# One term of the edge keys on GpSimd, key sums in PSUM, the activation table ahead of the loads, and another cut of the index arrays

## The chip, the cores and the metric

The kernel runs on one core of a Trainium2 chip. The metric is device time in microseconds: the median of several executions, and beside it the time of one profiled execution. The engines are TensorE (PE in the profile, its weight loads PEld), VectorE (DVE), ScalarE (ACT), GpSimd (POOL) and SyncE (SP); each runs its own instructions in order and waits on semaphores for the others. SyncE, ScalarE and GpSimd issue DMAs.

## The reference

```python
def reference(nodes, edges_src, edges_dst, w_msg, w_self):
    # nodes [4096, 256] f32, edges [262144] i64, weights [256, 256] f32
    self_out = nodes @ w_self
    msg = nodes[edges_src] @ w_msg
    agg = np.zeros((N, D), dtype=np.float32)
    np.add.at(agg, edges_dst, msg)
    return (self_out + agg).astype(np.float32)
```

Each of 262144 edges adds one row of `nodes @ w_msg` to the row of its destination.

## The kernel before

Every edge becomes one number, a key made of its destination's segment, its source's block of 128 and remainders of both. The keys are laid out as 128 partitions by 2048 columns and sorted by VectorE (min and max of columns that stand apart by a given distance, line 974), with turns of the layout through TensorE (line 1100) and ScalarE's copies (line 1104) between rounds. When the keys are sorted, VectorE makes one-hot matrices from them (lines 564 and 601), TensorE counts edges per destination and source block into a ring in PSUM (line 628), ScalarE copies the counts out (line 655), and TensorE multiplies them with the projected nodes (line 718). Stores go out from GpSimd.

The change lies in the first 20 us. The order of instructions on each engine is that of the program text (a manual schedule).

- The index arrays come in five pieces of columns, `PIECES` (line 67). SyncE issues the load of each piece's destinations `d64` (line 222), ScalarE that of the first four pieces' sources `s64`, SyncE that of the fifth (line 224). All are 64-bit; the lower halves are read with a stride.
- For each piece (lines 239 to 261) ScalarE makes three conversions: `seg` (line 244, from `d`), `blk` (line 247, from `s`) and `dst_p` (line 250, from `d`). VectorE then runs four instructions: `seg * step + blk` (line 253), the minimum with a bound plus `dst_p` (line 254), `low = blk * c + s` (line 255), and the sum of both (line 259), which is the key. `seg` and `blk` lie in `XS[0]` and `XS[1]`, the sums in the sort's buffers `XA[0]` and `XA[1]`, all in SBUF. The first sort instruction of line 974 reads the keys of all pieces.
- ScalarE's activation table is loaded in front of its first activation, so behind the four loads that it issues.
- GpSimd fills constants (lines 229 to 291) and runs 111 small memsets for a table (line 298), which SyncE sends to memory and reads back (lines 300 and 301). Then GpSimd issues the loads of the weights and the nodes (lines 305 to 313); the first of them is made to wait for `loaded`, the last conversion of the last piece. A cast of the identity follows (line 314). TensorE turns the nodes with it (line 349).

Of the kernel before, what the change touches and what calls it, by code (L numbers as in the profile page):

```python
# [9 lines left out]
P = 128  # L10
FP32 = mybir.dt.float32
BF16 = mybir.dt.bfloat16
I32 = mybir.dt.int32
# [4 lines left out]
ALU = mybir.AluOpType  # L18
AX = mybir.AxisListType
ACTF = mybir.ActivationFunctionType  # L20

BW = 512
SEG = 384
SHORT = 256
# [11 lines left out]
PARTS = 2  # L36
# [9 lines left out]
FP = 96  # L46
# [17 lines left out]
FILL = {8: 10, 32: 3}  # L64
PSUM0 = 0x2000000
SENT = float(1 << 24)
PIECES = (512, 512, 480, 320, 224)
TOP = 32767
SORT_A = [
    ('b', 419, 0),  # L70
# [59 lines left out]
def kernel(  # L130
# [9 lines left out]
    nc = tc.nc  # L140

    N, D = nodes.shape
# [3 lines left out]
    NCOL = E // P  # L146
    assert NCOL == 2048
    T = N // P
    G16 = NCOL // P

    const = ctx.enter_context(tc.tile_pool(name="const", bufs=1))
# [18 lines left out]
    ident = const.tile([P, P], FP32, name="ident")  # L170
    make_identity(nc, ident[:])

    wcat = feat.tile([P, 4, D], BF16, name="wcat")
# [5 lines left out]
    stt = nc.vector.scalar_tensor_tensor  # L179
# [7 lines left out]
    XA = [sortp.tile([P, FP + NCOL + BP], FP32, name=f"XA{i}") for i in range(2)]  # L187
    XS = [sortp.tile([P, TOT], FP32, name=f"XS{i}") for i in range(2)]
    id2 = sortp.tile([P, 2 * P], FP32, name="id2")
    id_bf = sortp.tile([P, P], BF16, name="id_bf")  # L190
# [5 lines left out]
    def muladd(out, in_, m, a):  # L196
        return nc.vector.tensor_scalar(
            out=out, in0=in_, scalar1=float(m), scalar2=float(a), op0=ALU.mult, op1=ALU.add
        )

    tab = const.tile([P, G16], I32, name="tab")
    per, per_short = SEG * NCOL // N // NB, SHORT * NCOL // N // NB
    ahead = FULL * (per - per_short)
# [12 lines left out]
    ld = []  # L216
    j = 0
    for h, m in enumerate(PIECES):
        d64 = ldp.tile([P, m], I64, name=f"d64_{h}")
        s64 = ldp.tile([P, m], I64, name=f"s64_{h}")  # L220
        c = slice(j, j + m)
        nc.sync.dma_start(d64[:], edges_dst.rearrange("(p j) -> p j", p=P)[:, c])
        q = nc.scalar if h < 4 else nc.sync
        q.dma_start(s64[:], edges_src.rearrange("(p j) -> p j", p=P)[:, c])
        ld.append((d64, s64, c))
        j += m
# [3 lines left out]
        nc.gpsimd.memset(x[:, FP + NCOL:], SENT)  # L230
    for h in range(2):
        nc.gpsimd.tensor_copy(out=id2[:, h * P:(h + 1) * P], in_=ident[:])
    seg = XS[0][:, 0:NCOL].bitcast(I32)
    blk = XS[1][:, 0:NCOL].bitcast(I32)
    dst_p = XR[0][:, 0:NCOL]
    step = SEG * (NB - 1) // (SEG - SHORT)
    top_b = (NSEG - 1 - 6) * step
    assert step * (SEG - SHORT) == SEG * (NB - 1) and TOT >= NCOL
    for d64, s64, c in ld:
        dlo = d64[:].bitcast(I32)[:, 0::2]  # L240
        slo = s64[:].bitcast(I32)[:, 0::2]
        key = XA[0][:, FP + c.start:FP + c.stop]
        low = XA[1][:, FP + c.start:FP + c.stop]
        nc.scalar.activation(
            out=seg[:, c], in_=dlo, func=ACTF.Copy, scale=1.0 / SEG, bias=0.5 / SEG - 6.5
        )
        nc.scalar.activation(
            out=blk[:, c], in_=slo, func=ACTF.Copy, scale=1.0 / P, bias=0.5 / P - 0.5
        )
        loaded = nc.scalar.activation(  # L250
            out=dst_p[:, c], in_=dlo, func=ACTF.Copy, scale=1.0 / (SEG - SHORT), bias=0.0
        )
        stt(out=key, in0=seg[:, c], scalar=float(step), in1=blk[:, c], op0=ALU.mult, op1=ALU.add)
        stt(out=key, in0=key, scalar=float(top_b), in1=dst_p[:, c], op0=ALU.min, op1=ALU.add)
        stt(
            out=low, in0=blk[:, c], scalar=float((SHORT - 1) * P), in1=slo, op0=ALU.mult,
            op1=ALU.add,
        )
        stt(
            out=key, in0=key, scalar=float((SEG - SHORT) * P), in1=low, op0=ALU.mult, op1=ALU.add  # L260
        )

    zer = const.tile([P, 3, P], BF16, name="zer")
    NAT = 20
    atr = const.tile([P, NAT, BW], BF16, name="atr")
# [10 lines left out]
    stgn = tc.alloc_tile_pool(name="stage_n", bufs=1)  # L276
# [13 lines left out]
    nc.gpsimd.tensor_copy(out=rows[:, 0:2 * NW], in_=jrow[:, ON_ACT:].rearrange("p k i -> p (k i)"))  # L290
    nc.gpsimd.tensor_copy(out=rows[:, 2 * NW:], in_=drow[:, 0:NW].rearrange("p k i -> p (k i)"))
    nc.sync.dma_start(kd[0:1, NCOL:NCOL + 1], ones_sent[:])
    c = 0
    for n, wid, gap in GROUPS:
        z = slice(c // GP, (c + n) // GP)
# [5 lines left out]
    nc.sync.dma_start(  # L301
        by_q[:], tab_d.rearrange("o (t h q) -> q (o t) h", t=3, h=PARTS)
    )
    DEP = mybir.DependencyInfo(mybir.DependencyClass.Sync, mybir.DependencyReason.DATA)
    first = nc.gpsimd.dma_start(wcat[:, 0:2, :], w_self.rearrange("(k p) f -> p k f", p=P))
    tc.add_manual_dep(first.ins, loaded.ins.name, DEP, reason="edges first")
    nc.gpsimd.dma_start(wcat[:, 2:4, :], w_msg.rearrange("(k p) f -> p k f", p=P))
    nodes_bf = stgn.tile([P, T, D], BF16, name="nodes_bf")
    for t in range(0, T, T // PARTS):
        nc.gpsimd.dma_start(  # L310
            nodes_bf[:, t:t + T // PARTS, :],
            nodes[t * P:(t + T // PARTS) * P, :].rearrange("(b p) f -> p b f", p=P),
        )
    nc.gpsimd.tensor_copy(out=id_bf[:], in_=ident[:])

    psum_y = tc.alloc_tile_pool(name="psum_y", bufs=1, space=bass.MemoryType.PSUM)

# [131 lines left out]
    for t in range(GP // 4):  # L449
        tp = psum_sort.tile([P, 512], FP32, name="tp_sw", tag="tp", bufs=4)  # L450
        for k in range(4):
            c = (4 * t + k) * P
            nc.tensor.matmul(
                out=tp[:, k * P:(k + 1) * P], lhsT=own[:, c:c + P], rhs=ident[:],
# [5 lines left out]
    for t, tp in enumerate(tps):  # L460
        for k in range(4):
            nc.tensor.matmul(
                out=tp[:, k * P:(k + 1) * P],
# [4 lines left out]
            out=vals[:].rearrange("p (q k) -> p q k", k=GP)[:, :, 4 * t:4 * t + 4],  # L468
            in_=tp[:].rearrange("p (k q) -> p q k", k=4),
            func=ACTF.Relu, scale=-1.0, bias=top[:],  # L470
        )

    def load(c):
        regs = [nc.tensor.alloc_register(f"po{c}_{i}") for i in range(NREG)]
        h, q = divmod(c // NREG, P)
        nc.tensor.load(regs, poff[q:q + 1, h * GP:h * GP + NREG])
        return regs
# [3 lines left out]
    first = load(0)  # L481
# [145 lines left out]
    def count_mm(ap, lhsT, rhs, start, after=()):  # L627
# [6 lines left out]
        for i in after:  # L634
            tc.add_manual_dep(mm, i.name, DEP, reason="bank free")
        tc.add_to_no_dep_group("count", mm)
# [14 lines left out]
    def evac(r):  # L651
# [6 lines left out]
        )  # L658
        tc.add_manual_dep(ins, last_mm[0].name, DEP, reason="run complete")
        tc.add_to_no_dep_group("evac", ins)  # L660
# [133 lines left out]
    if True:  # L794
# [5 lines left out]
        c = 0  # L800
# [5 lines left out]
        for c in range(NCOL):  # L806
# [44 lines left out]
            for _ in range(FILL.get(c + 1, 0)):  # L851
                nc.tensor.matmul(
                    out=out_ps[:, 2:4, :], lhsT=zw[:, 0:P], rhs=zw[:], start=True, stop=True,
                    skip_group_check=True,
                )
            while nev < NRUN and (evac_at(nev) <= c or c == NCOL - 1):
# [6 lines left out]
                if stores and nev % 4 == 0:  # L863
                    dst, src = stores.pop(0)
                    tc.add_manual_dep(
                        nc.gpsimd.dma_start(out=dst, in_=src, accum_op=ALU.add).ins,  # L866
                        evac_of[nev].name, DEP, reason="pace",
                    )
# [350 lines left out]
```

## Time and profile before

| | |
|---|---|
| median of 3 runs | 418.43 us (417.76 to 420.45) |
| the profiled execution, its own time | 418.17 us |
| span of that execution, first to last instruction | 416.4 us |
| mean granted clock of TensorE | 0.978 of full speed |
| first VectorE key instruction | 7.56 us from the span's start |
| first sort instruction | 19.18 us |

Times in the views are microseconds from the start of the span unless they are marked ns. "Idle before" is the time for which an engine stood idle ahead of an instruction, and behind the arrow is what released it.

### The profile page before, as it was taken

How to read it: one execution, taken by the hardware profiler on the slowest of the kernel's cores; microseconds unless marked ns; L12 is line 12 of the kernel's file. 1: busy time of each engine (PE TensorE's matmuls, PEld its weight loads, DVE VectorE, ACT ScalarE, POOL GpSimd, SP SyncE). 2: the span in 40 equal slices, each digit the busy share in tenths (PEclk: the TensorE clock that was granted, in tenths of full speed). 3: DMA queues.
4: the chain of work that ended last, by engine and by line, in shares of the span. 5: the costliest groups of instructions: out<-in, count | busy, mean ns of one | idle time of the engine just before them, and what ended most of it. 6: DMA issues, size and time to landing. Idle time of an engine off the chain costs nothing.

```text
span 416.4 us, 10756 instructions
## 1 busy us (share of the span) xinstructions
PE 335.5 (81%) x4128; PEld 287.9 (69%) x4137; DVE 374.9 (90%) x916; ACT 270.0 (65%) x559; POOL 43.0 (10%) x172
## 2 busy tenths in 40 slices
PE   0038477876967198999999998898988999999995
PEld 0025255564845056999999998797878988898895
DVE  6999999999799989999999999989997999998851
ACT  4328154553538015889888888996876877777782
POOL 8400000000000000002011020100102030202010
PEclk9999699999999689999999999999999999999999
DMA  8690000101023200003012020230203020211212
GB/s 305 138 185 4 2 1 2 50 0 52 1 101 116 87 0 2 2 2 39 2 16 28 2 32 10 53 41 8 33 3 39 2 32 12 28 14 15 29 16 53
DMA packets 18074, 16.20 MB, mean 39 GB/s; under 512 B 3684, under 2 KB 16997, under 8 KB 18022
## 3 DMA queue, kind: packets, MB, share of 16 engines
q0 software_dynamic: 8992, 6.29, 12.7%
q1 hardware_dynamic: 8310, 7.20, 5.3%
q10 hardware_dynamic: 720, 2.00, 1.2%
q8 instruction: 34, 0.56, 0.6%
q14 instruction: 18, 0.15, 0.1%
HBM read 8.93 MB, written 8.66 MB: 42 GB/s over the span
## 4 chain that ended last, share of the span: by engine, by line
DVE 47%; PE 45%; issue 3%; ACT 3%; DMA 1%; DVEq 0%; ACTq 0%
DVE XA L974 18%; PE out_ps L718 18%; PE ring L628 17%; DVE e_oh L601 7%; PE tp_sw L1100 5%; DVE d_oh L601 5%; DVE XS L974 4%; DVE XR L974 3%; DVE off L564 3%; PE warm L994 2%; PE out_ps L725 1%; DMA d<-in_edges_dst_dram 1%; ACT XA L1104 1%; DVE atr L688 1%; ACT atr L655 1%
## 5 line engine op out<-in xcount | busy, mean ns | idle before, releaser
L655 ACT CAST atr<-ring 128x472 bf16<-128x472 f32 (+11 forms) x352 | 177.2, 553 | 45.7 <-PE ring L628 40.7
L718 PE MATMUL out_ps<-Y,atr 128*128 128x256 bf16 x1024 | 162.2, 272 | 2.9 <-DVE atr L688 2.0
L628 PE MATMUL ring<-d_oh,e_oh 128*128 128x88 bf16 (+9 forms) x2048 | 149.7, 203 | 9.9 <-issue 4.5
L628 PEld LDWEIGHTS <-e_oh 128*128 128x128 bf16 x2048 | 129.2, 97 | 16.4 <-issue 9.7
L718 PEld LDWEIGHTS <-atr 128*128 128x128 bf16 x1024 | 90.7, 97 | 10.8 <-DVE atr L688 2.3
L974 DVE TENSOR_TENSOR XA<-XA 128x510 f32<-128x510 f32 (+30 forms) x154 | 89.3, 630 | 6.9 <-ACT XA L1104 5.3
L601 DVE TENSOR_SCALAR e_oh<-off 128x1024 bf16<-128x1024 int16 (+5 forms) x254 | 87.0, 402 | 7.9 <-PE ring L628 5.2
L628 PE MATMUL ring<-zer 128*128 128x158 bf16 (+12 forms) x352 | 81.4, 231 | 0.1
L866 POOL DMA_DIRECT2D out_dram<-o_sb x30 | 28.9, 963 | 357.8 <-ACT atr L655 357.8
L601 DVE TENSOR_SCALAR d_oh<-off 128x1024 bf16<-128x1024 int16 (+5 forms) x204 | 63.9, 373 | 0.0
L1104 ACT COPY XA<-tp_sw 128x512 f32<-128x512 f32 x32 | 20.9, 654 | 41.5 <-PE tp_sw L1100 41.2
L1100 PE MATMUL tp_sw<-XA,id 128*128 128x128 f32 x256 | 36.7, 298 | 7.9 <-DVE XA L974 7.8
L1100 PEld LDWEIGHTS tp_sw<-XA,id 128*128 128x128 f32 x256 | 33.1, 194 | 13.7 <-DVE XA L974 8.7
L564 DVE TENSOR_TENSOR off<-pair,rows 128x2048 int16<-128x2048 int16 (+5 forms) x34 | 38.6, 1134 | 0.3
L628 PEld LDWEIGHTS <-zer 128*128 128x128 bf16 x352 | 34.1, 97 | 5.0 <-ACT atr L655 1.9
L994 PE MATMUL warm<-zw 128*128 128x512 bf16 x61 | 20.8, 440 | 17.5 <-DVE XS L974 9.3
L349 PE MATMUL x_ps<-id_bf,nodes_bf 128*128 128x128 bf16 x64 | 8.5, 304 | 29.3 <-DMA nodes_bf<-in_nodes_dram 28.0
L725 PE MATMUL out_ps<-Y,atr 128*88 128x256 bf16 (+7 forms) x115 | 31.2, 272 | 0.0
L688 DVE TENSOR_TENSOR atr<-atr 128x178 bf16<-128x178 bf16 (+24 forms) x100 | 23.7, 260 | 6.4 <-ACT atr L655 6.0
L349 PEld LDWEIGHTS <-nodes_bf 128*128 128x128 bf16 x64 | 6.6, 139 | 30.9 <-DMA nodes_bf<-in_nodes_dram 28.3
L321 PE MATMUL y_ps<-wcat,XT 128*128 128x256 bf16 x128 | 21.7, 278 | 6.9 <-ACT Y L325 2.8
L592 ACT ACTIVATE e_oh<-off,onesc 128x512 bf16<-128x512 uint16 (+5 forms) x36 | 24.6, 686 | 2.7 <-DVE off L564 2.7
(114 smaller groups left out, 223.3 us busy)
## 6 DMA issues: line engine op xcount, KB each, us to landing
out_dram<-o_sb POOLq DMA_DIRECT2D x30, 128.0 KB, 3.2
nodes_bf<-in_nodes_dram POOLq DMA_DIRECT2D x2, 1024.0 KB, 12.6
out_dram<-nodes_bf SPq DMA_DIRECT2D x4, 512.0 KB, 2.9
out_dram<-XA SPq DMA_DIRECT2D x4, 512.0 KB, 3.0
d<-in_edges_dst_dram SPq DMA_DIRECT2D x2, 512.0 KB, 5.5
s<-in_edges_src_dram ACTq DMA_DIRECT2D x2, 512.0 KB, 5.7
d<-in_edges_dst_dram SPq DMA_DIRECT2D x1, 480.0 KB, 9.6
s<-in_edges_src_dram ACTq DMA_DIRECT2D x1, 480.0 KB
```

The costliest lines, as they stand in the source:

```text
L564: tt(out=v[:, 0:n // 2].rearrange("p g w (k i) -> p (g w) k i", i=2), in0=pair[:, g].rearrange("p g w i -> p (g w) i").unsqueeze(2).to_bro ...
L601: ins = tss(out=o[:, 0:n // 2, j:j + m].rearrange("p g k i -> p g (k i)"), in_=v[:, 0:n // 2, w, 0:2 * m], scalar=float((-j0 if w else ON_ ...
L628: mm = nc.tensor.matmul(out=ap, lhsT=lhsT, rhs=rhs, start=start, stop=True, skip_group_check=True,).ins
L655: ins = nc.scalar.copy(out=at[:, 0:n], in_=ring[:, b:b + n]).ins
L688: tt(out=atr[:, j:j + n, 0:m], in0=atr[:, j:j + n, 0:m], in1=atr[:, i:i + n, at:at + m], op=ALU.add,)
L718: nc.tensor.matmul(out=out_ps[:, i, :], lhsT=at[:, t * P:(t + 1) * P], rhs=Y[:, b, :], start=(b == 0 and not last and t % 2 == 0), stop=(b ...
L725: nc.tensor.matmul(out=out_ps[0:m, 0, :], lhsT=spill[:, c0:c0 + m], rhs=Y[:, b, :], start=False, stop=False, skip_group_check=True,)
L866: nc.gpsimd.dma_start(out=dst, in_=src, accum_op=ALU.add).ins,
L974: self.nc.vector.tensor_tensor(out=out, in0=in0, in1=in1, op=op),
L994: self.nc.tensor.matmul(out=w[:], lhsT=self.zw[:, 0:P], rhs=self.zw[:], start=True, stop=True).ins
L1100: self.nc.tensor.matmul(out=tp[:, g * P:(g + 1) * P], lhsT=self.turned(rots[8 * h + 4 * t + g]), rhs=sel(x)[:, 4 * t + g], start=True, sto ...
L1104: self.nc.scalar.copy(out=sel(y)[:, 4 * t:4 * t + 4], in_=tp[:].rearrange("p (g i b) -> p g i b", g=4, b=bb),)
```

## The change

One short activation (`early_c`), on a cell that VectorE's first instruction sets to zero, stands ahead of the loads, so the table is loaded first. The pieces have other sizes, and ScalarE issues the sources of all but the first piece. Conversions run `blk`, `seg`, `dst_p`. For pieces 1 and 2 (counted from 0) GpSimd makes `low` with two instructions, and there `seg` goes to PSUM and `blk` to SBUF; for the others `low` stays on VectorE, `blk` goes to PSUM and `seg` to SBUF. The running sum `run` is in PSUM for all. The last sum of a piece (`finish_keys`) stands where `KEY_ORDER` says: a number is a piece's first part, a number with `~` its last sum. The weights and nodes wait for the fourth piece's last conversion, and GpSimd's small memsets and the table's transfers come behind them.

```diff
-PIECES = (512, 512, 480, 320, 224)
+PIECES = (256, 512, 512, 480, 288)
+ON_POOL = (1, 2)
+KEY_ORDER = (0, ~0, 1, 2, ~1, 3, ~2, ~3, 4, ~4)
...
+    early_c = const.tile([P, 1], FP32, name="early_c")
+    nc.vector.memset(early_c[:], 0.0)
+    nc.scalar.activation(out=early_c[:], in_=early_c[:], func=ACTF.Copy, scale=1.0, bias=0.0)
...
-        q = nc.scalar if h < 4 else nc.sync
+        q = nc.scalar if h else nc.sync
...
-    for d64, s64, c in ld:
...
+    def parts(h):
...
+        run = psum_k.tile([P, BW], FP32, name="run", tag="run", bufs=3)[:, 0:m]
+        held = psum_k.tile([P, BW], I32, name="held", tag="held", bufs=2)[:, 0:m]
+        seg, blk = (held, part[:, c]) if h in ON_POOL else (part[:, c], held)
...
+        low = XA[1][:, FP + c.start:FP + c.stop].bitcast(I32)
+        if h in ON_POOL:
+            nc.gpsimd.tensor_single_scalar(
+                out=low, in_=blk, scalar=(SHORT - 1) * P, op=ALU.mult
+            )
+            nc.gpsimd.tensor_tensor(out=low, in0=low, in1=slo, op=ALU.add)
+        else:
+            stt(
+                out=low, in0=blk, scalar=float((SHORT - 1) * P), in1=slo, op0=ALU.mult,
+                op1=ALU.add,
+            )
+        stt(out=run, in0=seg, scalar=float(step), in1=blk, op0=ALU.mult, op1=ALU.add)
+        stt(out=run, in0=run, scalar=float(top_b), in1=dst_p[:, c], op0=ALU.min, op1=ALU.add)
+        runs[h], lows[h] = run, low
+        return last
+
+    def finish_keys(h):
+        c = ld[h][2]
+        stt(
+            out=XA[0][:, FP + c.start:FP + c.stop], in0=runs[h],
+            scalar=float((SEG - SHORT) * P), in1=lows[h], op0=ALU.mult, op1=ALU.add,
+        )
+
+    for what in KEY_ORDER:
+        if what >= 0:
+            loaded = parts(what)
+            if what == len(PIECES) - 2:
+                near_end = loaded
+        else:
+            finish_keys(~what)
...
+    tc.add_manual_dep(first.ins, near_end.ins.name, DEP, reason="edges first")
```

## Rows read from the trace of the kernel before

**Rows 1.** The page's busy time by engine, with shares and instruction counts.
```profile
PE 335.5 (81%) x4128; PEld 287.9 (69%) x4137; DVE 374.9 (90%) x916; ACT 270.0 (65%) x559; POOL 43.0 (10%) x172
```

**Rows 2.** The chain that ended last, 0 to 60 us: start, length, what.
```profile
0.77 5.53 DMA d<-in_edges_dst_dram
...
19.18 1.02 DVE XA L974
```

**Rows 3.** Timeline of ScalarE: start, length, instruction, count, idle before and releaser.
```profile
0.77 2.60 ACTq L224 DMA_DIRECT2D s<-in_edges_src_dram  x4
3.39 1.28 ACT L244 ACT_TABLE_LOAD   x1 [3.39 <-issue]
6.32 0.66 ACT L244 ACTIVATE XS<-d 128x512 int32<-128x512 int32 x1 [1.64 <-DMA d<-in_edges_dst_dram]
6.88 0.64 ACT L247 ACTIVATE XS<-s 128x512 int32<-128x512 int32 x1
...
8.88 0.67 ACT L244 ACTIVATE XS<-d 128x512 int32<-128x512 int32 x1 [0.80 <-DMA d<-in_edges_dst_dram]
...
11.31 0.64 ACT L244 ACTIVATE XS<-d 128x480 int32<-128x480 int32 x1 [0.64 <-DMA d<-in_edges_dst_dram]
...
14.19 0.38 ACT L244 ACTIVATE XS<-d 128x224 int32<-128x224 int32 x1
```

**Rows 4.** Timeline of VectorE, pieces of 512, 480 and 224 columns.
```profile
7.56 0.69 DVE L253 SCALAR_TENSOR_TENSOR XA<-XS,XS 128x512 f32<-128x512 int32 x1 [2.65 <-ACT XS L247]
8.36 0.69 DVE L254 SCALAR_TENSOR_TENSOR XA<-XA,XR 128x512 f32<-128x512 f32 x1
8.97 0.68 DVE L255 SCALAR_TENSOR_TENSOR XA<-XS,s 128x512 f32<-128x512 int32 x1
9.69 0.69 DVE L259 SCALAR_TENSOR_TENSOR XA<-XA,XA 128x512 f32<-128x512 f32 x1
10.30 0.68 DVE L253 SCALAR_TENSOR_TENSOR XA<-XS,XS 128x512 f32<-128x512 int32 x1
...
13.02 0.65 DVE L253 SCALAR_TENSOR_TENSOR XA<-XS,XS 128x480 f32<-128x480 int32 x1
13.78 0.66 DVE L254 SCALAR_TENSOR_TENSOR XA<-XA,XR 128x480 f32<-128x480 f32 x1
14.35 0.65 DVE L255 SCALAR_TENSOR_TENSOR XA<-XS,s 128x480 f32<-128x480 int32 x1
...
17.54 0.38 DVE L253 SCALAR_TENSOR_TENSOR XA<-XS,XS 128x224 f32<-128x224 int32 x1
18.03 0.39 DVE L254 SCALAR_TENSOR_TENSOR XA<-XA,XR 128x224 f32<-128x224 f32 x1
18.34 0.38 DVE L255 SCALAR_TENSOR_TENSOR XA<-XS,s 128x224 f32<-128x224 int32 x1
18.75 0.39 DVE L259 SCALAR_TENSOR_TENSOR XA<-XA,XA 128x224 f32<-128x224 f32 x1
```

**Rows 5.** The DMA view from 4 to 12 us: all packets.
```profile
DMA packets 1048, 3.27 MB, mean 409 GB/s; under 512 B 117, under 2 KB 163, under 8 KB 1047
```

**Rows 6.** Waits of SyncE's queue, 0 to 20 us: total, times, longest.
```profile
SPq L222 <- DMA s<-in_edges_src_dram: 3.5, 1, 3.5
```

**Rows 7.** Timeline of SyncE, the issue behind its loads.
```profile
9.26 0.30 SPq L292 DMA_DIRECT2D kd<-ones_sent  x1
```

**Rows 8.** VectorE's only read of PSUM, groups by shape: busy us, mean ns, idle before.
```profile
L742 DVE COPY XR<-out_ps 128x256 f32<-128x256 f32 x1 | 0.4, 424 | 4.3 <-PE out_ps L718 4.3
```

**Rows 9.** GpSimd's groups by shape that read 128 columns.
```profile
L314 POOL CAST id_bf<-ident 128x128 bf16<-128x128 f32 x1 | 0.9, 945 | 0.0
...
L232 POOL COPY id<-ident 128x128 f32<-128x128 f32 x2 | 0.5, 298 | 0.0
```

**Rows 10.** Timeline of GpSimd, the first load of weights.
```profile
15.48 0.89 POOL L305 DMA_DIRECT2D wcat<-in_w_self_dram  x1 [5.26 <-ACT XR L250]
```

**Rows 11.** Timeline of TensorE, the first work behind the projected nodes.
```profile
47.08 2.56 PE L994 MATMUL warm<-zw 128*128 128x512 bf16 x5 [5.32 <-DVE XA L974]
```

## What I expect of the change, blind

> **What bounds the kernel now.** I read the busy shares first, then the chain of waits, then the timelines of the first 20 us engine by engine, since every edit lies there. VectorE is the busiest engine, 90% of the span [rows 1]. The chain begins with the landing of the first destination indices (0.77 to 6.30) and from 19.18 it is VectorE's sort [rows 2]. Between the two stand ScalarE's conversions and VectorE's twenty key instructions. The reader should see two clocks there. Loads: ScalarE starts the first three pieces at 6.32, 8.88 and 11.31, each released by a landing [rows 3]. VectorE: it starts at 7.56 and issues four instructions for each piece without a gap to 19.18 [rows 4]. A piece of 512 columns takes it 2.74 us (7.56 to 10.30, the next piece's first start, which is one spacing of 0.61 behind 9.69), and the loads bring one in 2.56. So VectorE follows the loads closely, and what is taken from it can turn into waiting for data. That is what the sum has to decide. The sort behind it is one chain of VectorE work, so a shift of its start goes through to the end.
>
> **The table load and the smaller first piece.** ScalarE issues four loads from 0.77 to 3.37, then loads its table for 1.28 us, then is idle for 1.64 until the first destinations land [rows 3]: the table load costs nothing now. Moved ahead, it stands in front of the issues: 0.77 plus 1.28, plus one tiny activation (about 0.25, an estimate from the 0.38 of 224 columns, the smallest shape in [rows 3]), so the second piece's sources are issued at about 2.3. The tiny activation's memset goes ahead of VectorE's constants, about 0.1 us under the wait for data.
>
> When do pieces land? Destination landings at 6.32, 8.88 and 11.31 stand 512 and 480 columns apart: (11.31 - 6.32) / 992 = 5.0 ns for a column of both index arrays; all loads together ran at 409 GB/s [rows 5], so the pace is that of the transfers. The new pieces end at columns 256, 768, 1280, 1760 and 2048, on that line at 5.0, 7.6, 10.2, 12.6 and 14.05. Sources lag by a little: a SyncE issue was held until 9.26 by a source landing, when the destinations of the same piece had released ScalarE at 8.88 [rows 3, 7]. The third piece matters most. Its sources are the second load of ScalarE's queue. Before, the first 1024 columns of that queue landed by 9.24, 8.47 us behind the queue's first issue; the same columns behind an issue at 2.3 give 10.8, and the line plus 0.2 gives 10.4. I take 10.6, and keep both.
>
> [...]
>
> The tenth load now stands on ScalarE's own queue. The ninth load of the kernel before was held 3.5 us, until a load of the first piece had landed [rows 6], and I expect the same hold here, ahead of ScalarE's first conversion. It costs at most one issue, 2.60 / 4 = 0.65 us: the first conversion starts at 5.2 to 5.85. That is covered: VectorE's four instructions on 256 columns (some 0.42 us each, from 0.39 at 224) end by 8.1, and its next needs the second piece's two conversions, 7.8 + 0.57 + 0.65 = 9.0. If the cover were gone it would cost those 0.65.
>
> **What VectorE no longer does.** Two instructions of 512 columns go to GpSimd, at a spacing of 0.61 each: 1.2 us. The new order also parts some dependent pairs: starts are 0.80 and 0.72 apart where an instruction reads the one before it, 0.61 where not [rows 4]. Ten such pairs become seven, 3 x 0.15 = 0.4 us. With a start near 5.9 in place of 7.56, a count of VectorE's work alone would promise over 3 us.
>
> The data do not allow it. VectorE has two instructions for the second piece, from 9.05 to 10.5, and its next needs the third piece's two conversions: 10.6 + 0.57 + 0.65 = 11.8. It waits 0.9 us ahead of the second piece and 1.3 ahead of the third. From there twelve instructions remain, with the spacings of [rows 4] (512: 0.80 dependent, 0.61 free; 480: 0.76 and 0.57; 288, between the rows of 224 and 480: 0.56 and 0.48 dependent, 0.38 free, 0.45 to the sort): 0.80 + 0.61 + 0.61 + 0.57 + 0.76 + 0.57 + 0.61 + 0.57 + 0.38 + 0.56 + 0.48 + 0.45 = 6.97. The later pieces are in time: the fourth's first conversion is read at 13.8, and its data are due at 12.8; the fifth is read at 16.9 and is due at 14.3. Sort starts at 11.8 + 6.97 = 18.8, against 19.18: 0.4 us earlier (0.2 by the late landing, 0.6 by the early one).
>
> **Sums in PSUM.** All eighteen instructions now have one operand in PSUM. The trace has one VectorE read of PSUM: a copy of 256 columns took 424 ns [rows 8], while 224 columns from SBUF took 0.38 to 0.39 and 480 took 0.66 [rows 4], which is 0.42 for 256. So nothing is added, and I take nothing; a whole dependent spacing more (0.11 us) for each of the twelve would be 1.3 us, the upper bound. [...]
>
> **GpSimd's part.** Two instructions for each of two pieces. The nearest rows are copies of 128 columns at 298 ns, and a cast of as many at 945 ns that ran beside VectorE's sort [rows 9]. For 512 columns that is 1.2 to 3.8 us each. At 1.2 the first pair runs from 8.45 to 10.8 and the second from 11.2 to 13.6. VectorE wants them at 13.2 and 15.8, so it waits for neither. I take 1.2, since VectorE's key instructions now read one SBUF operand each, while the sort beside the slow cast reads two. [...]
>
> **What is moved.** The weights and nodes are released by the fourth piece's last conversion instead of the fifth's, about 0.7 us earlier than 15.48 [rows 10]. They feed TensorE's early work, which ended 5.32 us before its next job had to start [rows 11]: worth nothing, and covered if a late GpSimd delays it by as much. GpSimd's 111 small memsets now follow the nodes, and SyncE's two table transfers follow them; their reader comes only after the whole sort.
>
> **Rivals.** (A) VectorE is not starved, because its instructions or conversions are quicker than taken. The last data then bound it: 14.25 + 0.45 for the conversion + 0.38 + 0.56 + 0.48 + 0.45 = 16.6, so 2.6 us earlier and about 415.8. For it: 2.2 us of waits. Against it: those waits hang on transfers already at 409 GB/s. (B) ScalarE's queue starts late: issues held behind the table load for up to the 1.64 us that the trace shows idle there. At the full 1.64 the third piece lands at 12.2 and the sort starts at 20.4, 1.2 us later than now: about 419.6. It decides as soon as the issue is more than 0.4 us late. [...] (C) PSUM operands cost VectorE time: at half the upper bound, 0.65 us on twelve instructions, the start is 0.3 us later than now, about 418.7. (D) GpSimd is blocked beside VectorE as in the slow cast: four instructions at 3.8 us from 8.45 end at 23.6, and six VectorE spacings (3.0 us) follow, so the sort starts at 26.6: 7.4 us later, 425.8. It speaks from 1.8 us an instruction on, and passes 1% from about 3. Against it: one SBUF operand for VectorE.
>
> **Numbers.** The profiled execution took 418.17 around its span of 416.4, and the median of the runs is 418.43, so 0.26 more. 418.43 - 0.4 = 418.0. Chances: the forecast 0.58 (its own range 417.2 to 418.8), A 0.12, B 0.14, C 0.10, D 0.04, and 0.02 for a gain beyond A that I can't name. The range from 415.8 to 419.7 takes in A to C. About 1% (4.2 us) is what a measurement of this kernel can tell from no change: faster by more 0.02, within 0.94, slower by more 0.04 (D).
>
> **What would show it.** In the timeline of after: the first ScalarE load issue near 2.3 (B: up to 3.9); VectorE idle ahead of the first instructions of pieces two and three, released by ScalarE, about 1 us each (A: none); the last stretch of twelve without idle time, at today's durations (C: longer by 0.07 or more); GpSimd's four at about 1.2 us, done before the instructions that want them (D: VectorE waits on GpSimd); the first sort instruction near 18.8. The forecast is wrong if that start is off by more than 0.8, or if the rest of the kernel doesn't keep the shift.

## The result, and the profile after

The median is 421.42 us (420.73 to 422.23, six runs), against 419.01 for the kernel before in the same session: a ratio of 1.0066, 95% interval 1.0047 to 1.0085. The change makes the kernel 0.7% slower. That is within 1%, but above the predicted range (415.8 to 419.7) and 3.4 us from the forecast of 418.0. The profiled execution took 422.23 around a span of 420.4.

First the start. ScalarE's timeline of the kernel after: start, length, instruction, count, idle before and releaser.

```profile
0.74 1.28 ACT L205 ACT_TABLE_LOAD   x1 [0.74 <-PEq L1234]
0.92 1.34 ACTq L229 DMA_DIRECT2D s<-in_edges_src_dram  x3
2.04 0.20 ACT L205 ACTIVATE early_c<-early_c 128x1 f32<-128x1 f32 x1
6.93 0.33 ACTq L229 DMA_DIRECT2D s<-in_edges_src_dram  x1
7.31 0.40 ACT L284 ACTIVATE held<-s 128x256 int32<-128x256 int32 x1 [5.08 <-DMA s<-in_edges_src_dram]
...
9.65 0.62 ACT L287 ACTIVATE held<-d 128x512 int32<-128x512 int32 x1 [0.72 <-DMA d<-in_edges_dst_dram]
...
12.15 0.62 ACT L287 ACTIVATE held<-d 128x512 int32<-128x512 int32 x1 [0.74 <-DMA d<-in_edges_dst_dram]
...
15.44 0.45 ACT L287 ACTIVATE XS<-d 128x288 int32<-128x288 int32 x1
```

The issues of the second piece's sources did not wait for the table: three ran from 0.92, beside the load. But the small first piece, meant to come at 5.0, was taken at 7.31, and the destinations of the second and third at 9.65 and 12.15, where the line of 5.0 ns a column had 7.6 and 10.2. (The fourth issue, at 6.93, was held until the first piece had landed, its sources at 6.91, as foreseen; it stands between that landing and 7.31, and VectorE's work on the second piece did not wait for it.) VectorE's timeline of the same kernel:

```profile
7.75 0.42 DVE L300 SCALAR_TENSOR_TENSOR XA<-held,s 128x256 int32<-128x256 int32 x1 [2.93 <-ACT held L284]
...
10.31 0.70 DVE L304 SCALAR_TENSOR_TENSOR run<-held,XS 128x512 f32<-128x512 int32 x1 [0.79 <-ACT held L287]
11.12 0.70 DVE L305 SCALAR_TENSOR_TENSOR run<-run,XR 128x512 f32<-128x512 f32 x1
12.81 0.70 DVE L304 SCALAR_TENSOR_TENSOR run<-held,XS 128x512 f32<-128x512 int32 x1 [0.99 <-ACT held L287]
...
16.14 0.67 DVE L305 SCALAR_TENSOR_TENSOR run<-run,XR 128x480 f32<-128x480 f32 x1
...
18.80 0.47 DVE L305 SCALAR_TENSOR_TENSOR run<-run,XR 128x288 f32<-128x288 f32 x1
...
19.79 1.01 DVE L1005 TENSOR_TENSOR XA<-XA 128x815 f32<-128x815 f32 x1
```

Both waits of VectorE are there (0.79 and 0.99, predicted 0.9 and 1.3), released by ScalarE. From 12.81 nothing is idle: twelve spacings to 19.79 are 6.98 us, predicted 6.97. The sort starts 0.61 later than before [rows 2], not 0.4 earlier. (That start varies: over all profiles with the loads of before it is 18.79 to 19.18, with the loads of after 19.64 to 19.86. The 19.18 is the latest of its kind, so 0.6 to 0.9 is lost here.) GpSimd's timeline:

```profile
9.03 1.50 POOL L295 TENSOR_SCALAR XA<-XS 128x512 int32<-128x512 int32 x1 [2.61 <-ACT XS L284]
10.62 1.28 POOL L298 TENSOR_TENSOR XA<-XA,s 128x512 int32<-128x512 int32 x1
11.87 1.48 POOL L295 TENSOR_SCALAR XA<-XS 128x512 int32<-128x512 int32 x1
13.44 1.29 POOL L298 TENSOR_TENSOR XA<-XA,s 128x512 int32<-128x512 int32 x1
15.50 0.94 POOL L325 DMA_DIRECT2D wcat<-in_w_self_dram  x1 [0.78 <-ACT held L284]
```

Its last sum ends at 14.73, and VectorE reads it from 16.71 on, so VectorE never waited for GpSimd.

So 0.6 to 0.9 us of the loss is made before the sort. The spans differ by 4.0 in these two executions (420.4 and 416.4). About 1.1 us of that is the first turn through TensorE. The chains of waits, first of after, then of before:

```profile
50.25 3.39 PE tp_sw L1131 x16
```

```profile
49.63 2.29 PE tp_sw L1100 x16
```

The granted clock stood at 0.50 of full speed from 42.98 to 53.22 in after, and from 43.47 to 50.30 in before. The length of this stretch does not decide the time: among the experiments' profiles that record it, it ends at 51.03 in e2 (median 420.73) and at 52.27 in e16 (416.86), and of the six executions of after, the one with the highest mean granted clock (0.988) took 421.78 and one at 0.974 took 420.73. What remains arises late, in the counting stage. VectorE makes the one-hots' offsets there in 34 instructions (`off`, line 564 of before), which serve as marks: the delay of the same mark against before, in us, out of the timelines of some kernels, the experiments' among them (each is one execution):

| mark in before | 156.2 | 299.7 | 340.5 | 368.5 | 390.9 |
|---|---|---|---|---|---|
| after | +1.73 | +1.83 | +2.81 | +5.01 | +4.04 |
| e12, after once more | +1.53 | +1.68 | +1.14 | +3.51 | +3.29 |
| e10, after without one wait | +1.24 | +1.30 | +1.07 | +0.93 | +0.19 |
| e5, before with six warm-ups | -0.53 | -0.27 | -0.53 | -1.11 | -3.62 |
| e9, the same six later | +0.35 | +0.71 | -1.07 | -1.65 | -3.49 |
| e15, before with twelve | +0.34 | +0.63 | +0.25 | +0.74 | +0.61 |

For 144 us every row of the table is nearly flat: a shift is handed on there. (Three kernels outside the table, e4, e7 and e14, fall back by 1.6 us between 286.5 and 299.7; theirs are the only profiles with the granted clock at half there, for 3.4 us.) Between 300 and 391 us each row goes its own way, by up to 4 us, and what stood in a row at 299.7 does not tell where it ends. The windows view from 300 to 350 us (us, then busy time and instructions of PE, PEld, DVE, ACT, POOL, granted clock, DMA share, GB/s), before and after:

```profile
300.00:350.00 50.00, 45.87 (x684) 41.64 (x684) 44.84 (x133) 36.82 (x73) 5.89 (x6) 1.00 0.15 18
```

```profile
300.00:350.00 50.00, 44.36 (x656) 39.85 (x655) 44.02 (x133) 35.58 (x71) 6.19 (x6) 1.00 0.16 20
```

In these 50 us at full clock TensorE of after does 28 matmuls fewer (by the marks, its work lies 2 to 3 us further back). The waits in that window (total, times, longest) say at what. Before:

```profile
PE ring L628 <- issue: 2.0, 3, 1.2
PEld L628 <- issue: 2.6, 5, 1.4
PEld L718 <- issue: 1.2, 2, 0.7
```

After:

```profile
PE ring L659 <- issue: 3.5, 7, 1.3
PEld L659 <- issue: 5.0, 9, 1.4
PEld L749 <- issue: 0.3, 1, 0.3
```

"issue" is time in which TensorE waited for nothing that the profile shows. (PE and PEld rows lie over one another in time, so their totals are not added.) Neither the ring nor the one-hots were edited: the change put work only into the first 20 us.

### The profile page after: what moved, and what is told of

It reads as the page before. It is cut to its first block, busy times and chain, and to the rows that moved or that the text cites. A ratio compares the mean times of both kernels' runs of the same rounds, so it can differ in the third digit from the quotient of the medians.

```text
span 420.4 us, 10776 instructions
## 1 busy us (share of the span) xinstructions
PE 337.4 (80%) x4137; PEld 288.6 (69%) x4137; DVE 374.0 (89%) x915; ACT 270.1 (64%) x560; POOL 50.8 (12%) x176
## 4 chain that ended last, share of the span: by engine, by line
PE 47%; DVE 43%; issue 4%; ACT 2%; DMA 2%; SPq 0%; DVEq 0%; ACTq 0%
PE out_ps L749 19%; PE ring L659 19%; DVE XA L1005 18%; DVE e_oh L632 6%; DVE XS L1005 6%; PE tp_sw L1131 6%; DVE d_oh L632 4%; DVE off L595 3%; DMA d<-in_edges_dst_dram 2%; DVE XR L1005 2%; PE out_ps L756 2%; ACT XA L1135 1%; DVE atr L719 1%; PE warm L1025 1%; ACT atr L686 1%
## 5 line engine op out<-in xcount | busy, mean ns | idle before, releaser
L659 PEld LDWEIGHTS <-e_oh 128*128 128x128 bf16 x2048 | 129.2, 97 | 18.8 <-issue 12.1
L897 POOL DMA_DIRECT2D out_dram<-o_sb x30 | 31.8, 1060 | 355.7 <-ACT atr L686 355.7
L1131 PEld LDWEIGHTS tp_sw<-XA,id 128*128 128x128 f32 x256 | 34.2, 200 | 13.6 <-DVE XA L1005 8.6
```

What stands on the lines that cost most here:

```text
L659: mm = nc.tensor.matmul(out=ap, lhsT=lhsT, rhs=rhs, start=start, stop=True, skip_group_check=True,).ins
L1131: self.nc.tensor.matmul(out=tp[:, g * P:(g + 1) * P], lhsT=self.turned(rots[8 * h + 4 * t + g]), rhs=sel(x)[:, 4 * t + g], start=True, sto ...
```

## The experiments

Times are medians; each ratio is to the kernel before, run in the same session.

**Each part by itself.** The change with the nodes released by the last piece again (e1), with the old split of the sources over the queues (e2), without GpSimd (e3), and the kernel before with the early table alone (e8).

```diff
# e1, in after
-            if what == len(PIECES) - 2:
+            if what == len(PIECES) - 1:
# e2, in after
-        q = nc.scalar if h else nc.sync
+        q = nc.scalar if h < 4 else nc.sync
# e3, in after
-ON_POOL = (1, 2)
+ON_POOL = ()
# e8, in before
+    early_c = const.tile([P, 1], FP32, name="early_c")
+    nc.vector.memset(early_c[:], 0.0)
+    nc.scalar.activation(out=early_c[:], in_=early_c[:], func=ACTF.Copy, scale=1.0, bias=0.0)
```

> The changed kernel, but the weights and nodes wait for the last conversion of the fifth piece again. Theory nodes: TensorE's early work ends 0.7 us earlier than before (41.0 against 41.8), stands idle 6.26 us instead of 5.32 ahead of the warm-up matmuls, and so the first turn runs at half clock (3.39 us instead of 2.29). Then here the work ends some 1.2 us later than in the changed kernel, the first turn takes about 2.3, and the median falls by about 1.1, to 420.3. Rival, chance of phase: the time at which the clock rises does not hang on that gap; the first turn may fall either way and the median stays within 0.4 of 421.4.

> The changed kernel, but ScalarE issues the sources of the first four pieces and SyncE those of the fifth, as before; the table load stays ahead. Theory load order: SyncE's queue carries the destinations of pieces one and two behind both arrays of piece nought, beside ScalarE's queue that is already at piece one, so the third piece's destinations landed at 12.06 where I took 10.6. With the old split both arrays of piece nought land by about 5.2, the third piece's destinations by 10.4, VectorE's first instruction starts near 6.0 and the sort near 18.5 instead of 19.79: median about 1.2 lower, 420.2. Rival, GpSimd or PSUM: the start of the sort stays within 0.4 of 19.79.

> The changed kernel, but VectorE makes the term low of all pieces and GpSimd none; sums stay in PSUM, loads as in the changed kernel. Theory load order: VectorE waited 0.79 and 0.99 us for conversions ahead of pieces one and two. One of the two added instructions (piece one's) falls into the second wait, the other costs about 0.6: the sort starts at 20.2 to 20.5 and the median is 0.5 to 0.7 higher, about 422. Rival, GpSimd costs more than it saves: the sort starts no later than 19.8 and the median falls.

> The kernel before with one part of the change alone: the tiny activation, and so the table load, ahead of ScalarE's issues. The trace of the changed kernel shows the issues running beside the table load (from 0.92, the table from 0.74 to 2.02), so the loads and the sort's start stay within 0.1 of before and the median within 0.4 of 418.2. Rival, a cause behind the first 20 us: about 2 us of the changed kernel's loss are not in the start of the sort; if this part alone carries them, the median is 420 or more.

| run | time | ratio, 95% | sort starts |
|---|---|---|---|
| e1 | 420.44 | 1.0061 (1.0048 to 1.0074) | 19.83 |
| e2 | 420.73 | 1.0058 (1.0038 to 1.0079) | 19.40 |
| e3 | 421.75 | 1.0085 (1.0070 to 1.0099) | 19.77 |
| e8 | 418.23 | 1.0000 (0.9981 to 1.0019) | 18.78 |

None of the parts removes the loss. The early release of the nodes costs and brings nothing that the intervals show: e1's median is near the 420.3 expected, but the kernel before was faster in that session too, and the ratio is that of after. e2 took its first piece at 4.93, but its third only at 11.20, when the sources came, and its sort started at 19.40, not at the 18.5 expected. GpSimd's share saves nothing: e3 starts its sort at the same moment. Its VectorE timeline shows why:

```profile
9.44 0.68 DVE L300 SCALAR_TENSOR_TENSOR XA<-held,s 128x512 int32<-128x512 int32 x1
10.55 0.69 DVE L304 SCALAR_TENSOR_TENSOR run<-XS,held 128x512 f32<-128x512 int32 x1 [0.42 <-ACT XS L287]
...
11.96 0.68 DVE L300 SCALAR_TENSOR_TENSOR XA<-held,s 128x512 int32<-128x512 int32 x1
12.79 0.69 DVE L304 SCALAR_TENSOR_TENSOR run<-XS,held 128x512 f32<-128x512 int32 x1 [0.15 <-ACT XS L287]
```

The two instructions that came back to VectorE (9.44 and 11.96) fell into the waits, which shrank to 0.42 and 0.15. I had expected a start of 20.2 to 20.5 there; it was 19.77. The table alone (e8) brings nothing: its 18.78 is no more than the lower end of the starts that the loads of before give.

**The first turn.** If the half clock in the first turn were the cause, warm-ups that start earlier would mend it. Six more warm-up matmuls went ahead of the first turn (e4 in after, e5 in before, e7 in after with e2's split).

```diff
-WARM = [((2.7, 1.4), 3)] * 4 + [...]
+WARM = [((5.4, 4.0, 2.7, 1.4), 3)] + [((2.7, 1.4), 3)] * 3 + [...]
```

> The changed kernel, but the warm-up matmuls ahead of the first turn are four groups of three, begun some 2.7 us earlier (near 44.6 instead of 47.29). Theory clock: the first turn of the changed kernel ran at half clock until 53.22; with TensorE busy earlier the clock is full when the turn starts at 50.25, the turn takes about 2.1 instead of 3.39 and the median falls by 1.1 to 1.3, to about 420.2. Rival: the first turn is as long as before and the median stays within 0.4 of 421.4.

> The kernel before, with the same earlier warm-up groups ahead of the first turn as in the run e4_warm_early. That run was 3.1 us faster than the changed kernel, of which the late start of the sort is no part. Theory clock, same for both kernels: TensorE's granted clock rises at times that fall by chance against the warm-up, so the kernel before loses at its first turn as well in part of its executions, and this one gains 0.5 to 1.2: about 417.3. Theory clock, worse for the changed kernel: the first turn of the kernel before is at full clock nearly always, and this one stays within 0.4 of 418.2. If it gains as much as the changed kernel did (to about 415), the gain is not tied to the change at all.

> The changed kernel with the old split of the loads and the earlier warm-up together. Theory: the sort starts at 19.4, 0.2 later than before; the first turn is at full clock; the median lies 0.3 to 0.5 below the run e4_warm_early (sort at 19.64), near 417.9, so no faster than before by more than 0.5. Rival: the split costs elsewhere what it gains, and the median stays at 418.3 or above.

e4: 418.32 (1.0007, 0.9987 to 1.0027). e7: 418.74 (1.0000, 0.9974 to 1.0026). e5: 413.68 (0.9882, 0.9857 to 0.9907), the fastest kernel of this study and faster than both. e7 did not reach the 417.9 expected: the earlier start of its sort (19.50) brought nothing in the time. The gains (421.22 of e12 to 418.32 in after, 417.94 of its session to 413.68 in before) are too large for the first turn: e5 is 0.53 us earlier at the first mark and 3.62 at the last. So they too arise in the counting stage.

**The same six, ahead of the second turn** (e6 in after, e9 in before), where the clock of before is full anyway (from 50.30).

```diff
+WARM = [((2.7, 1.4), 3), ((5.4, 4.0, 2.7, 1.4), 3)] + [((2.7, 1.4), 3)] * 2 + [...]
```

> The changed kernel with the same six extra warm-up matmuls, but ahead of the second turn, where the granted clock is full anyway. Theory clock: no gain, median 421 to 421.8. Rival, TensorE's instruction supply: twelve more instructions ahead of the counting stage shift where its code arrives, and that, not the clock, gave the run e4_warm_early its gain; then this median falls to 419 or less.

> The kernel before with the six extra warm-up matmuls ahead of the second turn, where the granted clock is full. The run e5_before_warm gained 4.3 us with the same six ahead of the first turn, but its trace is only 0.53 us ahead where the counting stage begins, and the rest is gained behind 307 us. Theory code supply: what counts is where TensorE's instruction stream stands, twelve instructions further on, so this one gains most of it too: 415 or less, with the start of the counting stage within 0.5 of before. Theory clock: no gain, 417.5 to 418.5.

e6: 419.01 (1.0014, 0.9993 to 1.0036). e9: 415.20 (0.9922, 0.9897 to 0.9947). Most of the gain is there without any warmth to win. What the two places have in common is that all later instructions of TensorE stand twelve places further back in its program.

**One wait.** TensorE's program differs between before and after in one thing only: the sums in PSUM (`psum_k`) share banks with the later `psum_y`, so TensorE's first weight load waits on VectorE and ScalarE as well as on the nodes. That takes one instruction more at the head of its program; it is passed at 19.79 and TensorE's work begins at 26.92, so it delays nothing. (The pages' counts of all instructions show it: 10756 before and 10757 in e11, 10766 in e10 and 10767 in e12.) e10 gives `psum_y` banks of its own, in after; e11 adds such a wait to the kernel before; e12 is after with another comment.

```diff
# e10, in after: the pool's line moved up
+    psum_y = tc.alloc_tile_pool(name="psum_y", bufs=1, space=bass.MemoryType.PSUM)
     psum_k = tc.alloc_tile_pool(name="psum_k", bufs=1, space=bass.MemoryType.PSUM)
# e11, in before, at the first x_ps matmul
+                        for late_one in (loaded, keyed):
+                            tc.add_manual_dep(ins, late_one.ins.name, DEP, reason="one more wait")
```

> The changed kernel with the turns' PSUM pool laid out ahead of the key sums' pool, so the two don't share banks: TensorE's first weight load no longer waits for VectorE and ScalarE, and the one extra instruction that held these waits is gone from TensorE's stream. Theory code supply: that one instruction is the part of the loss behind the first 60 us, and the median falls by 1.5 to 2, to about 419.5. Rival: nothing changes, 421 to 421.8.

> The kernel before, with the same two waits (VectorE's last key, ScalarE's last conversion) on TensorE's first weight load: both have long passed when it runs, so no wait is longer, but TensorE's stream has one instruction more in front of everything. Theory code supply: 1.5 to 2 us slower, near 419.8. Rival: within 0.4 of 418.1.

> The changed kernel itself once more, beside the others on the same chip, to see how its first turn and its counting stage come out in another profiled execution. All theories: median 421 to 421.8. Theory clock chance: the first turn may be at full clock here (2.1 to 2.3 us) with the median no lower.

e10: 418.95 (1.0014, 0.9995 to 1.0033). e11: 419.57 (1.0038, 1.0023 to 1.0053). e12: 421.22 (1.0070, 1.0048 to 1.0091). Without the one instruction 2.3 us of the loss are gone, although the sort starts as late as in after (19.86); with it the kernel before loses 1.2 us. (e10 also changes the PSUM banks of some tiles, which no run tests apart; e11 changes none, so there the instruction stands alone.) The window from 300 to 350 us in e10:

```profile
300.00:350.00 50.00, 46.28 (x692) 41.90 (x690) 44.92 (x135) 37.15 (x73) 6.54 (x6) 1.00 0.16 18
```

This window is not the only place of the loss: e12 runs level with e10 at the mark 340.5 and loses behind it. Between the marks 354.5 and 368.5 the six kernels with the wait and without extra warm-ups all fall back against before, after by 1.8, e12 by 2.4, e1, e2, e3 and e11 by 0.8 to 2.0; the three others without it (e8, e10, e13) get ahead by 0.2 to 0.4. The late start of the sort does not divide them this way: e10 and e13 have it, e11 has not. The weight loads' waits there (total, times, longest) go the same way: before (352 to 370 us) and e10 (353 to 371), then after (355.5 to 373.5) and e12 (354 to 372):

```profile
PEld L628 <- issue: 1.3, 5, 0.4
```

```profile
PEld L658 <- issue: 1.6, 5, 0.6
```

```profile
PEld L659 <- issue: 2.5, 4, 1.2
```

```profile
PEld L659 <- issue: 3.1, 4, 1.4
```

**Warmth or place, and the landing.** Two and twelve more warm-ups in the kernel before (e14, e15), and all loads on one queue in e10, without (e13) and with the six (e16).

```diff
# e14: two more ahead of the second turn
+WARM = [((2.7, 1.4), 3), ((2.7, 1.4), 4)] + [((2.7, 1.4), 3)] * 2 + [...]
# e15: six more ahead of the second and of the third
+WARM = [((2.7, 1.4), 3)] + [((5.4, 4.0, 2.7, 1.4), 3)] * 2 + [((2.7, 1.4), 3)] + [...]
# e13, in e10; e16 is this with e6's edit
-        q = nc.scalar if h else nc.sync
+        q = nc.sync
```

> The kernel before with two more warm-up matmuls (four more TensorE instructions with their weight loads) ahead of the second turn; six there gave 3.2 us. If warmth is what gained: a third of that gain, 417.2 to 417.5, with the second turn shorter and the counting stage as before. If the place of the later instructions in TensorE's program is what counts: no third of anything; the waits put down to issue in the counting stage differ from before, their sum (before 10.5 and 4.5 us) moves with the time, and the time can be anywhere from 415 to 420.

> The kernel before with six more warm-up matmuls ahead of the second turn and six ahead of the third. If warmth is what gained: at least the 3.2 us of six, 413.5 to 415.2. If the place in TensorE's program counts: the gain is not kept by rule, 415 to 419, and its sum of issue waits in the counting stage lies between those of the kernel with six (time 415.2) and before by the same amount as the time.

> The changed kernel without the extra wait ahead of TensorE's first work (as in the run that takes it away), with all ten loads issued by SyncE, one behind the other, so that no second queue runs beside the first piece. If the late landing came from two queues that do not share the transfers equally: the third piece's destinations land at 10.2 to 10.8 instead of 12.1, the sort starts at 18.7 to 19.2 instead of 19.8, and the time is 418.0 to 418.4, 0.6 to 0.9 below the same kernel with two queues (418.95). If the transfers as a whole are simply slower with the smaller rows: the third piece lands near 12, the sort starts at 19.7 to 19.9 and the time stays at 418.9 to 419.1.

> The kernel with one load queue and without the extra wait, and six more warm-ups ahead of the second turn: TensorE's stream is the same as in the kernel before with those six (415.2). If place in TensorE's program counts, the gain of 3.2 carries over: 414.6 to 415.4, with the sort's start as in the run with one queue. If what the six gain depends on the data's timing instead, as the changed kernel with the six (419.0, a gain of 2.2 there) would have it: 415.8 to 416.4 or more.

| run | time | ratio, 95% | warm-ups more than before |
|---|---|---|---|
| e14 | 417.25 | 0.9962 (0.9935 to 0.9989) | 2 |
| e9 (above) | 415.20 | 0.9922 (0.9897 to 0.9947) | 6 |
| e15 | 420.44 | 1.0054 (1.0030 to 1.0078) | 12 |
| e13 | 419.66 | 1.0028 (1.0006 to 1.0050) | 0 |
| e16 | 416.86 | 0.9979 (0.9953 to 1.0006) | 6 |

Two fit warmth by the median (a third of six, 417.2 to 417.5), but not run by run: four of e14's twelve executions took 414.5 to 415.0 and the others 416.2 to 419.7, with one and the same program. Twelve refute it: 2.1 us slower than none, where warmth asked for 413.5 to 415.2. The windows view from 300 to 350 us, e9 and then e15:

```profile
300.00:350.00 50.00, 47.96 (x733) 44.31 (x731) 46.33 (x140) 38.91 (x78) 7.66 (x6) 1.00 0.16 18
```

```profile
300.00:350.00 50.00, 45.46 (x679) 41.43 (x680) 44.85 (x133) 36.11 (x72) 5.72 (x6) 1.00 0.15 18
```

Six put 49 matmuls more into these 50 us than the kernel before has, twelve 5 fewer. (The profiled execution of e15 took 418.41, near the 418.17 of before's, so it does not show the 2.1 us of the median.) That fits place. e16 was to reach 414.6 to 415.4 and came out at 416.86, outside it; but against its own base, e13 (419.66), six gained 2.8, nearly the whole 3.2. What was not kept is the base: e13, whose TensorE program is that of before, is 1.3 slower than before, of which its later sort (19.56) can be a part. So place alone doesn't set the time, and neither does it within one kernel, as e14 shows; what the other engines do at that moment may count too, which no run shows by itself.

e13 speaks on the landings. With one queue ScalarE's timeline has the pieces in order:

```profile
4.46 0.40 ACT L285 ACTIVATE held<-s 128x256 int32<-128x256 int32 x1 [2.22 <-DMA s<-in_edges_src_dram]
...
8.77 0.66 ACT L285 ACTIVATE XS<-s 128x512 int32<-128x512 int32 x1 [3.23 <-DMA s<-in_edges_src_dram]
...
11.36 0.67 ACT L285 ACTIVATE XS<-s 128x512 int32<-128x512 int32 x1 [0.84 <-DMA s<-in_edges_src_dram]
11.94 0.60 ACT L288 ACTIVATE held<-d 128x512 int32<-128x512 int32 x1
```

```profile
12.57 0.70 DVE L305 SCALAR_TENSOR_TENSOR run<-held,XS 128x512 f32<-128x512 int32 x1 [1.09 <-ACT held L288]
```

The first piece came at 4.46 instead of 7.31, the third at 11.36 instead of 12.15, and the sort started at 19.56, in e16 at 19.77: 0.1 to 0.3 earlier than in e10, not the 0.6 and more that I had expected if unequal sharing were all. The trace says where the gain went. The third piece's destinations had landed at 10.04, earlier than I had expected, but its sources, next in the one queue, at 11.33, and two conversions follow these (11.36 to VectorE's 12.57), where in after only one follows the destinations (12.15 to 12.81). So the piece was complete 0.8 earlier than in after, and VectorE began on it 0.24 earlier. The time did not follow: e13 and e10 cannot be told apart by their intervals.

## Why the prediction was wrong

**The landing term (10.6, measured 12.15).** This is the step that failed first. It cost 1.0 us at the sort's start (19.79 for 18.8, past the 0.8 that the prediction had set as a sign of being wrong), and not 1.55, because one of the two conversions that the prediction placed behind the landing was already done. The line of 5.0 ns a column [rows 3] took two things for granted: that all transfers together keep their pace, and that what lands is always the next piece, a fixed bit ahead. The windows view of the first microseconds, before and after (the last number is GB/s):

```profile
4.00:5.00 1.00, 0.00 (x0) 0.00 (x0) 0.84 (x5) 0.68 (x1) 0.87 (x3) 1.00 1.02 418
5.00:6.00 1.00, 0.00 (x0) 0.00 (x0) 0.00 (x0) 0.00 (x0) 0.94 (x2) 1.00 1.00 397
...
8.00:9.00 1.00, 0.00 (x0) 0.00 (x0) 0.89 (x3) 0.20 (x2) 1.00 (x32) 1.00 1.01 412
```

```profile
4.00:5.00 1.00, 0.00 (x0) 0.00 (x0) 0.78 (x4) 0.00 (x0) 0.87 (x3) 1.00 1.02 295
5.00:6.00 1.00, 0.00 (x0) 0.00 (x0) 0.00 (x0) 0.00 (x0) 0.93 (x2) 1.00 0.94 356
...
8.00:9.00 1.00, 0.00 (x0) 0.00 (x0) 0.90 (x3) 0.93 (x3) 0.00 (x0) 1.00 0.99 350
```

Summed over all rows of that view up to 9 us, before had moved 2.59 MB and after 2.36: 0.22 MB behind, about 0.55 us at 0.41 MB a microsecond. And more of what had moved belonged to later pieces. A column of both arrays is 2 KB. When before took its third piece (11.31) 3.52 MB had moved, of which the first 1504 columns are 3.08: 0.44 ahead of need. When after took its third (12.15) 3.66 had moved for 2.62 of need: 1.04 ahead. The 0.6 more is 1.5 us. Line plus both is 10.2 + 0.55 + 1.5 = 12.2, the measured 12.15. (This is bookkeeping of the same bytes and so has to close; it says how much each part took, not why.) Most of the lead comes with the second queue, as e13 shows below: the second and third pieces' sources shared the engines with the first piece. That ScalarE's issues at 0.92 came earlier than forecast (2.3) may have added to it; no run delays them alone. By 7 us SyncE's queue, which carried what VectorE waited for, had moved 0.66 MB and ScalarE's 0.88; with e2's split it was the other way round, 1.19 and 0.80 MB by 8 us, and the late one was again what was waited for. With one queue (e13) the lead fell from 1.04 to 0.60 MB, but the transfers were 0.36 MB behind by 9 us, which took part of the gain back. Why the rate dips (in after the median packet of 2 KB took 84 ns, that of 4 KB 159, which alone is 5%) stays open. So does why the two queues had moved 0.66 and 0.88 MB; no run shows how the engines share their time between queues.

**The table load.** "Stands in front of the issues" was wrong in the other direction: the issues ran beside it (0.92 to 2.26, the load 0.74 to 2.02). Rival B, with its late issue, did not happen; that the third piece landed near its 12.2 is a coincidence, and the sort started 0.6 before its 20.4. The activation behind this first load started at 2.04, 0.02 behind the load's end.

**Right.** The twelve spacings were right (6.98 for 6.97). So were sums in PSUM at no cost: 0.42 to 0.43 for 256 columns, 0.70 for 512, against 0.42 and 0.69 worked out or shown before [rows 4, 8], so rival C falls. GpSimd took 1.28 to 1.50 an instruction, near the 1.2 taken, and was waited for by nobody (D falls). No VectorE instruction beside GpSimd's is longer (0.68 to 0.70 for 512 columns in after, the same in e3 without GpSimd). The cast that took 945 ns beside the sort [rows 9] took 0.35 us in after (19.46 to 19.81), beside a key sum with one operand in SBUF. That the number of VectorE's SBUF operands makes the difference was my estimate; no run changes it alone. VectorE is starved as forecast, by 0.79 and 0.99 (A falls). The moved release of the nodes is worth nothing that the intervals show (e1 1.0061, after 1.0066).

**"A shift of its start goes through to the end."** This is the step that cost more: 2.3 of about 2.9 us. The prediction had no term for TensorE's program and carried every shift of the sort's start to the end. That holds up to 300 us, by the marks, and not beyond: e10 carried 1.24 us to the first mark and kept 0.19 at the last. e10 against e12 shows it in the changed kernel (same sort start, 2.3 us), e11 in the kernel before (1.2 us), and e5, e9, e14 and e15 show 1 to 4 us in both directions by nothing but more instructions early in TensorE's program. By medians, 418.35 plus 0.6 is e10's 418.95, about what the sort's start lost, and the wait brings it to e12's 421.22; that the 0.6 is the sort's start is within the intervals, and not more than that.

The likely mechanism is the supply of TensorE's program. The page of after has a queue for instructions, the larger of two, which I take for TensorE's, the engine with by far the most of them (PE and PEld 4137 each on that page):

```profile
q8 instruction: 34, 0.56, 0.5%
```

That is 34 packets of 16 KB. In the trace of after packets stand at 300.3, 309.1, 319.5 and 327.7 us, and TensorE's weight loads have their issue waits behind each, these the longest:

```profile
302.78 0.10 PEld L659 LDWEIGHTS <-e_oh 128*128 128x128 bf16 x1 [1.32 <-issue]
...
312.42 0.10 PEld L659 LDWEIGHTS <-zer 128*128 128x128 bf16 x1 [0.59 <-issue]
...
322.22 0.27 PEld L659 LDWEIGHTS <-e_oh 128*128 128x128 bf16 x5 [1.41 <-issue]
330.54 0.12 PEld L659 LDWEIGHTS <-e_oh 128*128 128x128 bf16 x2 [0.38 <-issue]
```

So here issue waits come in a group behind each packet of 16 KB, the longest 2.5 to 3.3 us behind it. If the boundaries between these blocks of program make the waits, one instruction more would move each of them by one instruction, and with it the place in a group of matmuls where TensorE stands still: it would be harmless where TensorE waits for a one-hot anyway, and lost where VectorE and ScalarE then wait in turn. What is shown is that a few instructions early in TensorE's program, even one, move the time by 1 to 4 us, nearly all of it behind 300 us, and that the longest of the waits stand 2.5 to 3.3 us behind the packets. The sum of the waits goes with the time: over all eighteen profiles, the matmuls' issue waits from 295 to 412 us are 2.1 to 3.0 us in the three executions of 414.8 to 416.2 us, 4.1 in before, and 5.8 to 6.9 in the five of 420.3 to 422.2 (correlation 0.88). It is not exact: e14 has 2.8 at 418.35. That the boundaries cause the waits, and what a moved wait does to the other engines, is argued, not shown, and why one instruction costs 2.3 us in after and 1.2 in before, or why one program has executions 4 us apart (e14), is open.

## What to carry to other kernels

When loads set the pace, count when each piece is complete and what still follows its last array, not how fast the bytes come: here a second queue started on later pieces, and by 7 us it had moved 0.88 MB and the one that was waited for 0.66. VectorE work taken away in front of a wait brought nothing (the sort starts at 19.79 without it and at 19.77 with it, e3). And one instruction more in TensorE's program, here a wait that a shared PSUM bank brought, moved the end by 2.3 us (e12 against e10) and by 1.2 (e11), nearly all of it 300 us later, where the edit was to gain 0.4; see what the edit adds to each engine's program, and try it with a few instructions more or less before judging it by 1%.

## What was not expected of the hardware

DMA issues on ScalarE's queue ran from 0.92 to 2.26, beside a table load from 0.74 to 2.02. Six matmuls of no use in TensorE's program made the kernel before 3.2 and 4.3 us faster (e9, e5), twelve 2.1 us slower (e15). GpSimd's `int32` product over 512 columns took 1.48 to 1.50 us, its sum 1.28 to 1.29, and VectorE's instructions of 512 columns took 0.68 to 0.70 with it (after) and without it (e3).
